# Loading the first adaLN weights ahead of the tokens, and another order of block 1's branches

## The chip, the cores and the metric

The kernel runs on one core of a Trainium2 chip. A core has TensorE (PE in the profile, with its weight loads as PEld), VectorE (DVE), ScalarE (ACT), GpSimd (POOL) and SyncE (SP, which here only issues DMAs). The metric is the device time of one execution in microseconds (us). Three runs of the kernel before took 3515.60, 3515.91 and 3515.91 us; the median is 3515.91.

## The reference

Three blocks follow each other on 512 tokens of width 1024, all in float32.

```
def reference(x, c, ctx, c_ctx, ...):
    x = first_block(x, c, ctx, c_ctx, ...)
    x = second_block(x, ...)
    return third_block(x, c_3, ...)

# first_block, one layer
sh1, sc1, g1, sh2, sc2, g2 = split(silu(c) @ w_ada + b_ada, 6)
p = modulate(rms_norm(x, norm1_g), sh1, sc1) @ w_in       # 10272 columns
q, k, v, a_dn, r, conv_in, sgu_in, gate_logit = split(p)
o = gla_bidir(q, k, v, gates(a_dn), s_f, s_b)             # 4 heads, chunks of 64, both directions
y_a = (rms(o) * gla_norm_g * silu(r)) @ w_o_gla           # attention branch
hc = depthwise_conv(c1 * sigmoid(c2))                     # 31 taps within rows of 64
y_b = silu(layer_norm(hc)) @ w_o_conv                     # convolution branch
y_c = (su * sp) @ w_o_sgu                                 # spatial gating branch
y = sigmoid(gate_0) * y_a + sigmoid(gate_1) * y_b + sigmoid(gate_2) * y_c
x = x + g1 * (y @ w_out)
x = x + g2 * swiglu(modulate(rms_norm(x), sh2, sc2))
```

The states `s_f` and `s_b` come from 256 context tokens with a modulation of their own. The second block has two layers, each a feed-forward, a mixer of two kinds of causal attention (8 heads with forget gates, 4 differential heads) and a feed-forward. The third block is one layer: a gated linear recurrence and block-sparse attention beside each other, one output projection.

## The kernel before

**Main products.** Activations lie as eight blocks of 128 features x 512 tokens. Each float32 factor is split into a rounded part `hi` and the rest `lo`, and a main product of a 128x128 weight tile is three matmuls: weight hi by activation hi, hi by lo, lo by hi (`mm3`; a triple below, 4408 in the kernel). The profile shows two of them with `whi` and one with `wlo`.

**Weights.** They stream in chunks of 128x1024 (512 KB, eight triples each) over SP's queue into three buffers `wraw`; ScalarE rounds a chunk to `whi`, and VectorE (in some stages POOL for every other chunk) subtracts to `wlo`. `w_start` issues the first loads, `w_ensure` the rounding, `w_finish` the subtraction and the next load; `wnext` calls the last two as triples go by.

**What sets the order.** Every engine executes its instructions in the order in which the program issues them. That order is made when the kernel is built, by a planner: a clock (`k.clk`) adds up planned times from small cost functions (`cost_pe`, `cost_act`, `cost_dve`, `cost_pool`). The side work (attention heads, the convolution, norms) is written as generators. After every triple `tick` lets each of them go on; `yield from k.sync()` holds one back until TensorE's planned time has passed the planned end of its last operation. So the planned costs decide behind which triple a dependent side matmul stands in TensorE's row. A matmul that stands too early makes TensorE wait, since the row is in order; one that stands late only delays what hangs on it. `k.filler` is a generator that is asked when little else is due: in block 1 `conv_work`, which issues 8 channel blocks of 31 steps each on VectorE (`calm` lets it go on while VectorE's planned time is less than 1.5 us ahead).

**Block 1.** First the modulation: `Ada1` computes shift and scale in four pairs of 256 columns. Pair 0 is done on TensorE (`rows`: 8 matmuls with a 2-column stationary side, a copy, 4 transposes), pairs 1 to 3 on VectorE for the tokens (`step`: eight multiply-adds of 128x512, then `sums`, four matmuls with a column of ones). `warm(k, n)` issues n matmuls that compute nothing. Six columns of units (the convolution's first inputs, `first_units`) run over all eight blocks `m` while pairs 1 to 3 come in; then the rest of the convolution's inputs, queries, values and keys. Behind the keys the attention's generators start (`ctx_state`, `gla_heads` with two heads at a time, `conv_norm` for the layer norm behind the convolution), and the main units follow a list:

```
ORDER_1 = (some("r", range(KT)) + some("g", range(6), 1) + some("g", range(6), 0) + between(1, 6) + some("a", [0])
           + between(0, 6) + some("v", range(2)) + some("s", range(KT)) + some("g", range(6), 2) + between(2, 6))
```

`r` are the eight units of the attention's output gate, `(g, m, b)` a gate unit of branch b (0 attention, 1 convolution, 2 spatial gating), `p` a product of branch b, which needs all eight blocks of its source, `a` is a marker after which the gating of the attention may be finished, `v` and `s` are the inputs of the spatial gating. `between(b, ahead)` alternates products with the gate units that are still missing. A unit is eight triples. The attention of a head (`gla_head`, `gla_dir`, `gla_gate`) is a chain over all engines: log-sigmoid on ScalarE, scans on VectorE, products with the decay on POOL, small matmuls on TensorE, and so on; `both` is a 128x4 product of chunk decays in it.

**Lines.** Nearly every instruction is recorded on the helper's line (L256 before, L260 in the changed kernel; DMAs L247 and L251), so rows are told apart by tiles: `wraw`, `whi`, `wlo` weights, `b` blocks in SBUF, `bk` PSUM banks, `pvt` a table of parameters (the convolution's taps among them), `cst` constants, `small` and `tinies` columns.

## Time and profile before

| | us |
|---|---|
| median of three runs | 3515.91 |
| the profiled execution | 3511.07 |
| its span in the trace | 3509.3 |
| TensorE busy | 3405.3 |
| VectorE busy | 1911.7 |
| ScalarE busy | 1351.7 |
| POOL busy | 720.5 |

The rows below come from the profiled execution. Busy time is the time in which an engine executes; "idle before" is its idle time just ahead of an instruction, put down to the engine whose semaphore came last. [...] Stages by time: 0 to 83 us the start with its modulation, to 271 us the convolution's inputs, queries, keys and values, to about 520 us the attention of block 1 (beside its main units), to 840 us the branch products, and block 1's feed-forward behind them; the mixers of block 2 at 1640 to 1900 us and 2660 to 2900 us; block 3's mixer at 3290 to 3480 us.

### The profile page before, as it was taken

What the parts mean: (1) busy time and instruction counts of PE and PEld (TensorE: products, weight loads), DVE (VectorE), ACT (ScalarE), POOL (GpSimd) and SP (SyncE); (2) the same over time, 40 slices, a digit from 0 to 9 for tenths busy, and PEclk for the clock granted to TensorE, in tenths of its full rate; (3) what the DMA queues carried; (4) which work ended last, traced back from release to release, by engine and by line L of the source; (5) the groups of instructions that cost most, each with busy time, mean ns of one, the idle gap of its engine ahead of it and who ended that gap; (6) DMA issues with size and microseconds to landing.
All of it is one profiled execution on the core that took longest, in us unless ns stands there. A gap on an engine that the chain in (4) does not pass through costs nothing.

```text
span 3509.3 us, 39437 instructions
## 1 busy us (share of the span) xinstructions
PE 3405.3 (97%) x15210; PEld 2763.3 (79%) x15210; DVE 1911.7 (54%) x3010; ACT 1351.7 (39%) x2176; POOL 720.5 (21%) x564
## 2 busy tenths in 40 slices
PE   7998889999999999999999999999999999999999
PEld 5886678887888888887778888888887778888777
DVE  5899865655333365433686443344335774433566
ACT  3324462223322332324764222233227653232474
POOL 0004231222000101103452110011016331111362
PEclk9998999999999999999999999999999999999999
DMA  6211114543322244232122222322332123222221
GB/s 209 93 56 55 48 49 149 181 156 102 102 98 99 99 159 164 97 117 98 55 68 80 99 97 96 96 96 97 107 108 72 60 68 108 96 96 96 72 79 55
DMA packets 110189, 344.99 MB, mean 98 GB/s; under 512 B 13425, under 2 KB 13681, under 8 KB 110001
## 3 DMA queue, kind: packets, MB, share of 16 engines
q1 hardware_dynamic: 84960, 296.78, 25.2%
q10 hardware_dynamic: 23760, 41.50, 3.7%
q0 software_dynamic: 1280, 4.20, 0.4%
q8 instruction: 119, 1.95, 0.2%
q14 instruction: 70, 0.57, 0.1%
HBM read 336.13 MB, written 6.29 MB: 98 GB/s over the span
## 4 chain that ended last, share of the span: by engine, by line
PE 52%; DVE 4%; ACT 2%; POOL 1%; issue 1%; DVEq 0%; POOLq 0%; ACTq 0%
PE bk L256 52%; DVE b L256 3%; ACT b L256 1%; DVE tinies L256 1%; POOL b L256 1%; POOL wlo L256 0%; DVE wlo L256 0%; ACT whi L256 0%; ACT L251 0%; ACT bk L256 0%; ACT tinies L256 0%; DVE small L256 0%; DVEq L256 0%; POOLq L256 0%; ACTq L256 0%
## 5 line engine op out<-in xcount | busy, mean ns | idle before, releaser
L256 PE MATMUL bk<-b,whi 128*128 128x512 f32 (+1 forms) x8048 | 2514.7, 394 | 6.8 <-ACT whi L256 3.4
L256 PEld LDWEIGHTS bk<-b,whi 128*128 128x128 f32 x8048 | 1506.7, 190 | 323.3 <-issue 9.6
L256 PE MATMUL bk<-b,wlo 128*128 128x512 f32 (+1 forms) x4024 | 1575.4, 391 | 6.7 <-DVE wlo L256 5.9
L256 POOL TENSOR_TENSOR b<-b,b 128x512 f32<-128x512 f32 (+2 forms) x381 | 528.4, 1395 | 2391.1 <-DVE b L256 1189.4
L256 DVE TENSOR_TENSOR wlo<-wraw,whi 128x1024 fp32r<-128x1024 f32 x495 | 643.8, 1303 | 528.8 <-ACT whi L256 528.5
L256 PEld LDWEIGHTS bk<-b,wlo 128*128 128x128 f32 x4024 | 762.2, 189 | 170.1 <-DVE wlo L256 8.8
L256 ACT CAST whi<-wraw 128x1024 fp32r<-128x1024 f32 x542 | 568.0, 1049 | 739.8 <-PE bk L256 442.8
L256 ACT CAST b<-b 128x512 fp32r<-128x512 f32 (+3 forms) x286 | 176.0, 618 | 523.9 <-POOL b L256 369.9
L256 DVE TENSOR_TENSOR b<-bk,b 128x512 f32<-128x512 f32 (+6 forms) x324 | 208.1, 659 | 253.7 <-PE bk L256 212.9
L256 DVE TENSOR_TENSOR b<-b,b 128x512 fp32r<-128x512 f32 (+3 forms) x250 | 184.7, 745 | 251.0 <-ACT b L256 248.9
L256 PE MATMUL bk<-b,b 128*128 128x128 f32 (+9 forms) x1056 | 250.4, 354 | 33.2 <-POOL b L256 20.4
L256 ACT ACTIVATE b<-b 128x512 f32<-128x512 f32 (+1 forms) x259 | 153.4, 608 | 308.7 <-DVE b L256 273.1
L256 PEld LDWEIGHTS bk<-b,b 128*128 128x128 f32 (+3 forms) x1056 | 174.1, 193 | 109.9 <-issue 36.0
L256 PE MATMUL bk<-whi,b 128*128 128x512 f32 x768 | 248.4, 397 | 4.0 <-ACT b L256 2.2
L256 DVE SCALAR_TENSOR_TENSOR b<-b,pvt,b 128x392 f32<-128x392 f32 (+7 forms) x296 | 229.0, 778 | 33.3 <-ACT b L256 26.4
L256 PEld LDWEIGHTS bk<-whi,b 128*128 128x128 f32 x768 | 145.6, 190 | 36.6 <-DVE b L256 3.0
L256 DVE SCALAR_TENSOR_TENSOR b<-b,small,b 128x512 f32<-128x512 f32 (+1 forms) x178 | 148.0, 833 | 20.8 <-ACT b L256 15.5
L256 POOL TENSOR_TENSOR wlo<-wraw,whi 128x1024 fp32r<-128x1024 f32 x47 | 116.0, 2467 | 202.3 <-ACT whi L256 175.7
L256 PE MATMUL bk<-wlo,b 128*128 128x512 f32 x384 | 150.8, 393 | 0.0
L256 PE MATMUL bk<-cst,b 128*128 128x128 f32 (+1 forms) x776 | 111.5, 271 | 36.3 <-DVE b L256 25.3
L256 PEld LDWEIGHTS bk<-cst,b 128*128 128x128 f32 x776 | 98.9, 168 | 60.4 <-DVE b L256 31.8
L256 ACT ACTIVATE b<-bk 128x512 f32<-128x512 f32 (+2 forms) x170 | 97.2, 572 | 111.6 <-PE bk L256 109.9
(93 smaller groups left out, 1233.9 us busy)
## 6 DMA issues: line engine op xcount, KB each, us to landing
wraw<-in_wst SPq DMA_DIRECT2D x542, 512.0 KB, 3.3
b<-in_ada1r ACTq DMA_DIRECT2D x64, 256.0 KB, 4.4
b<-in_ada ACTq DMA_DIRECT2D x48, 256.0 KB, 4.1
b<-in_ada SPq DMA_DIRECT2D x32, 256.0 KB, 5.5
xpark<-b ACTq DMA_DIRECT2D x16, 256.0 KB, 2.0
b<-xpark POOLq DMA_DIRECT2D x16, 256.0 KB, 5.2
b<-in_x SPq DMA_DIRECT2D x8, 256.0 KB, 5.2
b<-in_x ACTq DMA_DIRECT2D x8, 256.0 KB, 4.5
```

The costliest lines, as they stand in the source:

```text
L256: return f(*a, **kw)
```

## The change

The diff in full:

```diff
--- before.py
+++ after.py
@@ -225,13 +225,17 @@
     n = width(out)
     if op == "reciprocal":
         return 0.07 + 6.4e-3 * n
+    if op == "tensor_tensor_scan":
+        return 0.03 + 2.2e-3 * n
+    if op == "scalar_tensor_tensor" and n > 300 and len(tuple(out.shape)) == 3:
+        return 0.2 + 1.1e-3 * n
     if op in ("tensor_scalar", "memset"):
         return max(0.2, 0.1 + 0.7e-3 * n)
     return max(0.2, 0.08 + 1.05e-3 * n)
 
 
 def cost_pool(op, out, a, kw):
-    return 0.06 + (1.0e-3 if op == "memset" else 2.3e-3) * width(out)
+    return 0.06 + 1.0e-3 * width(out) if op == "memset" else max(0.5, 0.1 + 2.7e-3 * width(out))
 
 
 class Engine:
@@ -1876,8 +1880,8 @@
     return o
 
 
-ORDER_1 = (some("r", range(KT)) + some("g", range(6), 1) + some("g", range(6), 0) + between(1, 6) + some("a", [0])
-           + between(0, 6) + some("v", range(2)) + some("s", range(KT)) + some("g", range(6), 2) + between(2, 6))
+ORDER_1 = (some("r", range(KT)) + some("g", range(KT), 0) + some("g", range(KT), 1) + some("a", [0]) + between(0, KT)
+           + between(1, KT) + some("v", range(2)) + some("s", range(KT)) + some("g", range(6), 2) + between(2, 6))
 
 
 def plan1():
@@ -1980,9 +1984,15 @@
     def rows(self, q):
 
         k, nc = self.k, self.k.nc
-        b, row = k.bank(), k.blk()
+        b = k.bank()
         for t in range(KT):
             nc.tensor.matmul(b[0:2], lhsT=self.sc[:, t, :], rhs=self.ws[q][t].f, start=t == 0, stop=t == KT - 1)
+        k.free(self.ws.pop(q))
+        return b
+
+    def turn(self, q, b):
+        k, nc = self.k, self.k.nc
+        row = k.blk()
         nc.scalar.copy(row.f[0:2], b[0:2])
         k.unbank(b)
         b = k.bank()
@@ -1991,7 +2001,7 @@
         for c in range(2):
             self.finish(q, c, b[:, c:8:2])
         k.unbank(b)
-        k.free(row, self.ws.pop(q))
+        k.free(row)
 
     def step(self, q, c, t, acc):
         ve, w, s = self.k.nc.vector, self.ws[q][t].f, self.sc[:, t, c:c + 1]
@@ -2138,7 +2148,7 @@
                          start=True, stop=True)
     pairs = lambda ap: ap.rearrange("p (b c t) -> p b c t", c=2, t=64)
     chunk = dec.rearrange("p (b c) -> p b c", c=2)
-    nc.gpsimd.tensor_mul(both, chunk[:, :, 0], chunk[:, :, 1])
+    nc.vector.tensor_mul(both, chunk[:, :, 0], chunk[:, :, 1])
     f, l = pairs(kd.f)[:, :, s], pairs(qe.f)[:, :, 1 - s]
     nc.gpsimd.tensor_mul(f, f, chunk[:, :, 1 - s:2 - s].to_broadcast([P, 4, 64]))
     nc.gpsimd.tensor_mul(l, l, chunk[:, :, s:s + 1].to_broadcast([P, 4, 64]))
@@ -2431,18 +2441,23 @@
     w = "w_in"
     st = dict(q={}, k={}, v={}, r={}, o={}, ck={}, cv={}, s0=[k.blk() for _ in range(4)], cdone=0, hdone=0,
               conv={}, hc={}, yb={}, z={}, sv={})
+    ada = Ada1(k)
+    ada.load(0)
     for m in range(KT):
         x.append(k.blk())
         nc.sync.dma_start(x[m].f, k.a["x"][:, m, :])
-    ada = Ada1(k)
-    ada.load(0)
+    k.w_start(1)
+    ada.load(1)
     k.w_start()
-    ada.load(1)
-    warm(k, 7)
+    row = ada.rows(0)
+    warm(k, 3)
     k.clk.t = k.clk.c["dve"] = k.clk.c["act"] = 6.0
     acc = sumsq(k, [x[m].f for m in range(KT)], S, nc.vector)
     lt, ly = rms_cols(k, acc.f, S, EPS1)
-    ada.rows(0)
+    ada.turn(0, row)
+    k.w_ensure(0)
+    k.w_finish(0)
+    warm(k, 3)
     bcb = bc_rows(k, ly)
     hx = []
 
@@ -2456,8 +2471,6 @@
         k.free(x[m])
 
     prepare(0)
-    k.w_ensure(1)
-    k.w_finish(1)
     prepare(1)
     ada.load(2)
     cols = k.bank()
@@ -2474,7 +2487,7 @@
             summed = k.clk.t
         for n, c0 in enumerate(first_units()):
             k.main_mm3(fb[n], k.wnext(w, 0, m, c0), (hx[m][0].r, hx[m][1].r), m == 0, m == KT - 1)
-            if m % 2 == 1 and n == 1 and q < 4:
+            if m % 2 == 1 and n == 3 and q < 4:
                 k.clk.t = summed
                 ada.sums(cols[:, 4 * q:4 * q + 4], gacc)
                 ada.finish(q, 0, cols[:, 4 * q:4 * q + 4])
```

In words. (1) The planned costs of a scan, of a wide fused operation over three dimensions (the convolution's steps) and of every POOL operation change, and with them the places of side work in all three blocks. (2) In block 1 all 16 gate units of the attention and the convolution branch stand behind `r`, and the products of the attention branch come ahead of the convolution branch's. (3) The loads of ada pair 0 are issued ahead of the tokens, one weight chunk ahead of pair 1 and the other two behind it; the rows of pair 0 are the first work of TensorE; there are 3 + 3 warming matmuls instead of 7; the second weight chunk is finished later and the column sums of pairs 1 to 3 stand behind two more triples. (4) `both` moves from POOL to VectorE, 8 instructions.

The next two pieces are VectorE's row in the start of block 1: token blocks (`b_5` and `b_6` before, `b_13` and `b_14` after) times the broadcast norm in a bank, subtractions for their lo parts, weight halves (`wlo`), and the steps of ada pair 1 (into `b_51`, `b_52`). Before:

```order
L256 TENSOR_TENSOR b_5_95<-b_5_95,bk_70 128x512
L256 TENSOR_TENSOR b_40_222<-b_5_95,b_39_221 128x512
L256 TENSOR_TENSOR wlo_86<-wraw_80,whi_83 128x1024
L256 TENSOR_TENSOR wlo_87<-wraw_81,whi_84 128x1024
L256 TENSOR_TENSOR b_6_97<-b_6_97,bk_70 128x512
L256 TENSOR_TENSOR b_42_234<-b_6_97,b_41_233 128x512
L256 TENSOR_SCALAR b_51_254<-b_21_134,small 128x512
L256 SCALAR_TENSOR_TENSOR b_51_254<-b_22_135,small,b_51_254 128x512
```

After, from the second token block on; the half `wlo_86` and the second warming's memset stand ahead of this:

```order
L260 TENSOR_TENSOR b_14_117<-b_14_117,bk_71 128x512
L260 TENSOR_TENSOR b_43_232<-b_14_117,b_42_231 128x512
L260 TENSOR_SCALAR b_52_252<-b_21_132,small 128x512
L260 SCALAR_TENSOR_TENSOR b_52_252<-b_22_133,small,b_52_252 128x512
L260 SCALAR_TENSOR_TENSOR b_52_252<-b_23_134,small,b_52_252 128x512
L260 SCALAR_TENSOR_TENSOR b_52_252<-b_24_135,small,b_52_252 128x512
L260 SCALAR_TENSOR_TENSOR b_52_252<-b_25_136,small,b_52_252 128x512
L260 SCALAR_TENSOR_TENSOR b_52_252<-b_26_137,small,b_52_252 128x512
L260 SCALAR_TENSOR_TENSOR b_52_252<-b_27_138,small,b_52_252 128x512
L260 SCALAR_TENSOR_TENSOR b_52_252<-b_28_139,small,b_52_252 128x512
L260 TENSOR_TENSOR wlo_87<-wraw_81,whi_84 128x1024
L260 TENSOR_TENSOR wlo_88<-wraw_82,whi_85 128x1024
```

The half `wlo_87` of the second weight chunk stood ahead of the steps and stands behind the eighth of them.

The next two are TensorE's row during block 1's attention, where the sum over all convolution outputs (`cst` by the block with the accumulated sum, four matmuls of one column) stands. Before (this is behind triple 426, counted from the first):

```order
L256 MATMUL bk_73<-b_197_2574,b_183_2327 128x256
L256 MATMUL bk_69<-b_117_1365,b_185_2329 128x256
L256 MATMUL bk_67<-b_198_2577,b_187_2376 128x256
L256 MATMUL bk_72<-b_118_1366,b_189_2378 128x256
L256 MATMUL bk_71<-cst,b_111_1107 128x1 x4
L256 MATMUL bk_68<-b_64_317,whi_85 128x512
L256 MATMUL bk_68<-b_65_318,whi_85 128x512
L256 MATMUL bk_68<-b_64_317,wlo_88 128x512
```

After (behind triple 499):

```order
L260 MATMUL bk_71<-b_242_3066,b_217_2803 128x256
L260 MATMUL bk_73<-b_128_1623,b_219_2805 128x256
L260 MATMUL bk_66<-b_243_3069,b_224_2849 128x256
L260 MATMUL bk_72<-b_127_1622,b_226_2851 128x256
L260 MATMUL bk_67<-b_65_325,whi_85 128x512
L260 MATMUL bk_67<-b_66_326,whi_85 128x512
L260 MATMUL bk_67<-b_65_325,wlo_88 128x512
L260 MATMUL bk_68<-cst,b_112_1143 128x1 x4
L260 MATMUL bk_67<-b_67_331,whi_85 128x512
```

The side matmuls of attention heads (`b` by `b`) stand ahead of the sum in both; the sum stands 73 triples further on in the row.

The last two are the end of the attention in block 3, TensorE's row from its last attention matmuls (into `bk_73` before, `bk_70` after) to the next triples. Before:

```order
L256 MATMUL bk_73<-b_1808_22540,b_1634_21061 128x256
L256 MATMUL bk_73<-b_1809_22541,b_1634_21061 128x256
L256 MATMUL bk_73<-b_1808_22540,b_1632_21055 128x256
L256 MATMUL bk_73<-b_1809_22541,b_1632_21055 128x256
L256 MATMUL bk_68<-b_1779_22279,whi_83 128x512
L256 MATMUL bk_68<-b_1780_22280,whi_83 128x512
L256 MATMUL bk_68<-b_1779_22279,wlo_86 128x512
L256 MATMUL bk_70<-b_1760_22176,whi_84 128x512
L256 MATMUL bk_70<-b_1761_22177,whi_84 128x512
L256 MATMUL bk_70<-b_1760_22176,wlo_87 128x512
```

After:

```order
L260 MATMUL bk_71<-b_1807_22578,whi_85 128x512
L260 MATMUL bk_71<-b_1808_22579,whi_85 128x512
L260 MATMUL bk_71<-b_1807_22578,wlo_88 128x512
L260 MATMUL bk_70<-b_1811_22600,b_1635_21065 128x256
L260 MATMUL bk_70<-b_1812_22601,b_1635_21065 128x256
L260 MATMUL bk_70<-b_1811_22600,b_1633_21059 128x256
L260 MATMUL bk_70<-b_1812_22601,b_1633_21059 128x256
L260 MATMUL bk_73<-b_1813_22631,whi_85 128x512
```

Behind the last attention matmul 33 triples are left before and 20 after, to the end of the program.

## Rows read from the trace of the kernel before

**Rows 1.** page, busy time by engine: share, instructions

```profile
PE 3405.3 (97%) x15210; PEld 2763.3 (79%) x15210; DVE 1911.7 (54%) x3010; ACT 1351.7 (39%) x2176; POOL 720.5 (21%) x564
```

**Rows 2.** windows: length, busy us and instructions by engine, granted clock, DMA

```profile
83.20:271.20 188.00, 187.01 (x895) 156.87 (x894) 168.39 (x261) 50.81 (x75) 0.00 (x0) 1.00 0.24 78
271.20:400.00 128.80, 102.16 (x438) 79.46 (x438) 124.94 (x148) 56.42 (x119) 63.35 (x53) 0.87 0.14 47
400.00:519.50 119.50, 106.18 (x520) 87.91 (x519) 85.10 (x152) 78.96 (x147) 31.60 (x32) 0.93 0.15 49
...
1640.00:1900.00 260.00, 251.22 (x1103) 189.06 (x1103) 187.73 (x459) 166.67 (x365) 127.18 (x100) 0.96 0.19 64
...
2660.00:2900.00 240.00, 232.28 (x1027) 174.40 (x1026) 177.62 (x442) 157.35 (x355) 117.57 (x96) 0.96 0.19 64
...
3290.00:3480.00 190.00, 183.91 (x836) 143.83 (x835) 127.60 (x254) 128.28 (x230) 87.70 (x68) 0.98 0.21 69
```

**Rows 3.** waits of TensorE, 271.2 to 519.5 us: total, times, longest

```profile
PE bk L256 <- POOL b L256: 19.3, 10, 3.3
PE bk L256 <- DVE b L256: 16.9, 4, 7.9
```

**Rows 4.** groups of VectorE, 160 to 480 us: count, busy us, mean ns, idle

```profile
L256 DVE SCALAR_TENSOR_TENSOR b<-b,pvt,b 128x480 f32<-128x480 f32 (+14 forms) x222 | 168.0, 757 | 6.5
L256 DVE TENSOR_TENSOR wlo<-wraw,whi 128x1024 fp32r<-128x1024 f32 x33 | 43.4, 1314 | 2.0 <-ACT whi L256 2.0
L256 DVE TENSOR_TENSOR b<-b,b 128x512 f32<-128x512 f32 (+3 forms) x31 | 26.1, 857 | 3.4 <-ACT b L256 2.9
L256 DVE TENSOR_TENSOR_SCAN b<-cst,b 128x256 f32<-128x256 f32 (+1 forms) x16 | 20.4, 1282 | 1.3 <-POOL b L256 1.3
```

**Rows 5.** groups of TensorE, 271.2 to 519.5 us, matmuls with lo weights

```profile
L256 PE MATMUL bk<-b,wlo 128*128 128x512 f32 (+1 forms) x176 | 72.4, 412 | 0.6 <-DVE wlo L256 0.6
```

**Rows 6.** timeline of TensorE: start, length, idle before and releaser

```profile
422.54 0.39 PE L256 MATMUL bk<-b,wlo 128*128 128x512 f32 x1
...
423.89 0.39 PE L256 MATMUL bk<-b,wlo 128*128 128x512 f32 x1
...
454.57 1.87 PE L256 MATMUL bk<-cst,b 128*128 128x1 f32 x8 [7.92 <-DVE b L256]
```

**Rows 7.** POOL's groups by form, 160 to 480 us and 1900 to 2640 us

```profile
L256 POOL TENSOR_TENSOR b<-b,b 128x512 f32<-128x512 f32 x32 | 49.7, 1577 | 61.9 <-ACT b L256 46.0 <-DVE b L256 15.9
...
L256 POOL TENSOR_TENSOR b<-b,b 128x512 f32<-128x512 f32 x58 | 74.8, 1290 | 645.3 <-DVE b L256 399.9 <-ACT b L256 245.4
```

**Rows 8.** timeline of the start, all engines

```profile
6.39 4.17 SPq L247 DMA_DIRECT2D b<-in_ada  x8
...
6.61 4.26 ACT L256 ACTIVATE b<-b 128x512 f32<-128x512 f32 x8
...
7.40 8.56 PE L256 MATMUL bk<-b 128*128 128x512 f32 x14 [7.40 <-DVE b L256]
...
16.67 7.03 PE L256 MATMUL bk<-b,small 128*2 128x512 f32 x16
...
29.24 2.36 DVE L256 TENSOR_TENSOR wlo<-wraw,whi 128x1024 fp32r<-128x1024 f32 x2 [0.24 <-ACT whi L256]
...
29.26 1.22 PE L256 MATMUL bk<-b,whi 128*128 128x512 f32 x2 [3.41 <-ACT whi L256]
...
40.59 1.87 PE L256 MATMUL bk<-cst,b 128*128 128x1 f32 x8 [3.84 <-DVE b L256]
```

**Rows 9.** waits of TensorE, 3290 to 3480 us

```profile
PE bk L256 <- POOL b L256: 4.9, 1, 4.9
```

**Rows 10.** groups by form, 3290 to 3480 us, all engines

```profile
L256 POOL TENSOR_TENSOR b<-b,b 64x512 fp32r<-64x512 f32 x16 | 22.5, 1409 | 1.1
...
L256 DVE TENSOR_TENSOR b<-bk,b 64x512 f32<-64x512 f32 x7 | 4.8, 685 | 0.9 <-ACT b L256 0.7
...
L256 ACT COPY b<-bk 64x512 f32<-64x512 f32 x7 | 4.1, 582 | 4.1 <-PE bk L256 3.9
```

## The prediction

> **What bounds the kernel now.** I read the page first: TensorE is busy in 97% of the span [rows 1]. So only two things can be won: time in which TensorE waits, and time in which it runs at the lower of its two clocks. The windows say where that is [rows 2]. From 83.2 to 271.2 us TensorE is busy for 187.01 of 188 us at granted clock 1.00. In the next two windows, which are the attention of block 1, it is busy for 102.16 of 128.80 us and 106.18 of 119.50 us, at 0.87 and 0.93. These 248.3 us lose 39.9 us to idling. [...] At full clock without waits TensorE's work there would fill 208.3 - 25 = 183 us (up to 65 us lost). What it waits for there is POOL, 19.3 us, and DVE, 16.9 us [rows 3]. DVE is at its limit in the first of the two windows (124.94 of 128.80 us) and POOL is half full. The list of DVE's groups says with what: 222 steps of the depthwise convolution at 757 ns are 168 us, weight halves 43.4 us [rows 4]. So the stretch is bound by VectorE, because the convolution must be finished there: the matmul that sums its result stands early. The three attention stages of the later blocks lose less: 8.8, 7.7 and 6.1 us idle at clocks 0.96 to 0.98 [rows 2].
>
> **Block 1: other units during attention.** The window holds 176 triples (the row of lo weights counts one per triple) [rows 5], and at full clock one takes 0.68 us (two last matmuls of triples start at 422.54 and, two triples on, at 423.89 us) [rows 6]. In the order of before the sum over the convolution stands behind triple 426, that is 90 triples into the attention, and the first product (of the convolution branch) at triple 496. After the change the sum stands behind triple 499, and the first product (now of the attention branch) at triple 528; triples counted from the first main product. All products of a branch need all eight blocks of its source. So what has to be done by VectorE before TensorE may go on is spread over 192 triples (336 to 528) rather than 90, and the wait for the convolution's sum should go.
>
> What does VectorE do in those 192 triples? I counted the instructions between the two weight halves in the order of after and multiplied by the durations of before: 131 convolution steps x 757 ns = 99.2 us; 25 weight halves x 1314 = 32.9 us; 20 products of 512 at 857 = 17.1 us; 16 scans x 1282 = 20.5 us [rows 4]; the other 90 or so, small ones, about 42 us by their shapes, an estimate. Sum 212 us. TensorE's own work there is 183 + 16 x 0.68 = 194 us. So VectorE stays the limit, but by 18 us, not by 60. At the 97% at which the trace shows it at most (124.94 of 128.80) that takes 219 us. The convolution starts the stretch with 22 steps less behind it (101 instead of 123), so VectorE was less loaded before and may enter up to two weight chunks ahead; I take 5 us of these 11. That gives 214 us. Before, the same 192 triples took 248.3 + 16 x 0.68 = 259 us. **Gain: 45 us**, of which I count 44, since the sum over the convolution's squares comes later too.
>
> Its bounds: if TensorE's 194 us plus 10 us of short waits decide, 55 us are won. If POOL's chain (19.3 us of waits [rows 3]) isn't loosened by more triples between, 45 - 20 = 25.
>
> Heads 2 and 3 now run beside convolution steps. In the trace POOL's 512-wide products take 1577 ns in the stretch in which VectorE is full and 1290 ns in a stretch without convolution [rows 7]. Some 16 such products stand in heads 2 and 3: 16 x 0.29 = 4.6 us on POOL, which lies beside main products. I cost it at nothing; uncovered it is 5 us. [...]
>
> The eight tiny products that move from POOL (with `both`) to VectorE relieve POOL's chain by less than 1 us per head and add the same order to VectorE; counted in the 42 us above.
>
> **The start.** The first ada pair goes ahead of the tokens on SP's queue. Its eight loads take 4.17 us to issue, so the last token block lands 4 to 5 us later and the squares end at about 16 us instead of 10.87 [rows 8]. TensorE does the rows of pair 0 (7.03 us) meanwhile rather than after 14 halves of warming (8.56 us) [rows 8], of which 6 are left ahead of the sums. From 17 us: the sums, the inverse root and finishing the rows, 4 us together, as before; a weight half 1.2 and a memset 0.5 that the second warming waits for; that warming 6/14 x 8.56 = 3.7; broadcast, multiplication and scaling 2.7, as before. That makes the first main product start at 29.1 us instead of 29.26. The weight half of the second chunk, which stood ahead of the ada steps, now stands behind the eight of them (before, both halves start at 29.24 us [rows 8], ahead of the steps); TensorE needs it at triple 8. The steps start earlier by its 1.2 us and by the first half's 1.2 us, and the column sum, which came at 40.59 [rows 8], comes two main products later. From there VectorE paces the remaining pairs as before. Net 0, between -2 and +2 us.
>
> **Blocks 2 and 3: the planner's costs.** Higher planned costs for POOL, scans and the wide fused operations make the planner put dependent side matmuls later in TensorE's row. This takes a wait away where the real time was longer than the planned one. There is little to take: POOL's one wait in block 3 is 4.9 us [rows 9], and the two layers of block 2 idle for 16.5 us for all reasons; I put the upper gain at 10 us. What it costs is that the attention's side work ends nearer to the end of its cover. In block 3 the last attention matmul has 20 triples behind it instead of 33, and these 20 include the ones that need its result. That chain behind it is a copy of 0.58 us, an addition of 0.69 us, a POOL product of 1.41 us [rows 10], a cast and a subtraction of about 0.6 and 0.7 us: 4 us, with the clock's fall 5. The two layers of block 2 end their attention 4 and 6 triples later, with the same kind of chain: 3 us each. And in layer 2, 67 side matmuls now stand in one cluster between two triples where 21 stood; I put 1 us on it. **Sum +12 us.** The bounds: -10, and +40 where the chains of all three stages stand open at half clock and the waits of before remain (their whole loss today is 22.6 us idle and, by the clock of the windows, up to 24 us [rows 2]).
>
> **The sum.** -44 + 0 + 12 = -32 us against the profiled execution's 3511.07 us: 3479. That execution lies 4.8 us below the median of 3515.91; so 3484 on the median's footing. I take 3482.
>
> **The rivals.**
> A. The later blocks lose nothing or gain: the side matmuls that were moved had slack anyway. For it: TensorE idles only 3% to 4% there. Against it: the cover behind block 3's attention shrinks from 33 to 20 triples. Then 3516 - 45 = 3471, or 3461 with all POOL waits gone. I put 3468.
> B. Attention in block 1 stays bound more tightly than VectorE's sum says, by POOL's chains or by waits of VectorE for ACT in order: gain 25, and +12 later: 3503. For it: POOL waits are the larger part today. Against it: they were counted while VectorE, which feeds POOL, was late.
> C. Slower: VectorE works in order, and the change puts some 39 more convolution steps between the operations of heads 2 and 3: 39 x 0.757 = 30 us. If the last heads' outputs, ready at about 522 us before, come that much later, the first attention product, which needs all eight of them, holds TensorE until 552 us instead of passing at 485 us; before, TensorE was at this triple at 530. That is +22, and +12 from the later blocks makes 3550. It decides from outputs later than 518 us on. Against it: the heads start at the same triple, and the stretch ahead of them is shorter by the waits that go.
> D. The change doesn't move the end: what block 1 gives, the later blocks and the hole at 840 us take. 3513.
>
> **How the numbers follow.** What a measurement of this kernel can tell from no change is 0.2%, 7 us. Forecast 0.44, A 0.22, B 0.23, C 0.06, D 0.05. Forecast and A are faster by more than that, and of B all but 0.02: faster 0.87; D and the rest of B are 0.07 the same; C is 0.06 slower. The range leaves out C, D and the end of A in which every gain comes together (55 won and 10 more): 3456 to 3507.
>
> **What would show it.** In the window of heads 0 to 3 the idle of TensorE must fall from 39.9 us to under 15 and the clock rise to 0.97 or more, with VectorE at about 95% over it; the wait of 7.92 us before the convolution's sum [rows 6] must be gone, and the first product of the attention branch start at 480 to 492 us. If it starts later than 505, B holds; later than 530, C. At the start the first main product stands within 2 us of 29.26. In block 3 the 4.9 us behind POOL stays or shrinks, and a new wait of 3 to 6 us on the last attention blocks appears ahead of the last 20 triples; if none appears there and the windows of block 2 idle as before, A holds. Wrong altogether would be a new long wait in block 2's clusters, of more than 10 us in one place.

## The result, and the profile after

The changed kernel takes 3492.94 us (median of four runs, 3489.29 to 3493.59) against 3515.88 us: a ratio of 0.9933, with an interval of 0.9916 to 0.995. It is faster by 23 us, more than the 7 us that can be told from no change. Forecast were 3482 us and a range of 3456 to 3507: the direction and the range hold, and the gain is two thirds of the 34 us forecast. The profiled execution took 3493.36 us with a span of 3491.6 us, against 3509.3 us.

To see where the time went I counted triples: each has one matmul with lo weights, 4408 in every trace, so the start of the n-th of them is a common ruler. The table gives the difference in its start, changed kernel minus before, in us.

| triple | where | before starts at | difference |
|---|---|---|---|
| 0 | first main product | 30.52 | +3.5 |
| 8 | first with the second weight chunk | 43.32 | +0.1 |
| 100 | all ada pairs done | 121.53 | +6.7 |
| 336 | the attention of block 1 begins | 271.86 | +5.5 |
| 480 | inside it | 489.64 | -48.4 |
| 528 | first product in the changed order | 532.04 | -22.3 |
| 560 | products under way | 553.80 | -18.9 |
| 1024 | block 1's feed-forward | 902.72 | -22.2 |
| 2300 | behind layer 1's mixer | 1891.24 | -24.8 |
| 3650 | behind layer 2's mixer | 2919.59 | -20.5 |
| 4407 | last | 3505.12 | -17.7 |

So the start loses 6.7 us, the attention of block 1 gives 24.4 us (336 to 560), the rest of block 1 another 3 us, and blocks 2 and 3 take 4.5 us back. The lateness of the first product is made up by triple 8; the 6.6 us that stay are lost between triples 8 and 100. These are the windows of that stretch, first before, then in the changed kernel (columns as in the next table of windows):

```profile
43.32:121.53 78.21, 72.46 (x318) 59.43 (x316) 56.46 (x86) 29.11 (x39) 0.00 (x0) 0.94 0.38 124
```

```profile
43.47:128.28 84.81, 78.26 (x325) 63.01 (x325) 58.36 (x89) 28.25 (x38) 0.00 (x0) 0.88 0.39 131
```

TensorE idles 6.6 us instead of 5.8; the other 5.8 us are busy time, some 5 us of it by the granted clock, 0.88 instead of 0.94 (an estimate from these two rows: 0.12 x 84.81 us less 0.06 x 78.21 us). The granted clock stands in the profile as a share of full speed. Of 6980 windows of 0.5 us in the kernel before, 6676 read 1.00 and 264 read 0.50; a value between is a mean over a window in which it changes. These are the windows of the changed kernel for the convolution's inputs, the two halves of block 1's attention and the three later mixers (the last three set 20 us earlier than those of before, as the stages are). The columns are as in [rows 2]: length, busy us of TensorE, its weight loads, VectorE, ScalarE and POOL with instructions, the granted clock, DMA share and GB/s.

```profile
83.20:271.20 188.00, 188.00 (x890) 157.70 (x890) 159.16 (x246) 54.94 (x80) 0.00 (x0) 1.00 0.25 84
271.20:400.00 128.80, 116.46 (x543) 93.84 (x542) 119.98 (x152) 62.95 (x129) 58.58 (x49) 0.95 0.17 56
400.00:519.50 119.50, 107.49 (x533) 87.70 (x531) 99.11 (x167) 68.55 (x131) 33.98 (x27) 0.97 0.18 60
1620.00:1880.00 260.00, 249.56 (x1116) 189.21 (x1115) 187.00 (x461) 164.80 (x364) 124.44 (x100) 0.98 0.20 67
2640.00:2880.00 240.00, 228.42 (x1010) 171.03 (x1008) 178.10 (x438) 153.88 (x350) 114.71 (x93) 0.96 0.19 62
3270.00:3460.00 190.00, 186.24 (x847) 146.07 (x846) 133.21 (x253) 123.47 (x224) 86.21 (x67) 0.99 0.20 68
```

In the attention's 248.3 us TensorE idles 24.3 us where it idled 39.9 [rows 2], the clock is 0.95 and 0.97 instead of 0.87 and 0.93, and VectorE is busy for 93% and 83%. The reader is to see that VectorE isn't full in the second half: something else holds TensorE there. Its waits in the same 248.3 us, which answer to [rows 3] (total, times, longest):

```profile
PE bk L260 <- POOL b L260: 9.8, 7, 3.4
PE bk L260 <- ACT b L260: 7.8, 2, 7.4
PE bk L260 <- DVE tinies L260: 3.6, 2, 3.4
PE bk L260 <- DVE wlo L260: 2.0, 1, 2.0
PE bk L260 <- DVE b L260: 1.0, 2, 0.9
```

The waits for POOL halved, those for blocks of VectorE all but went, and a wait of 7.4 us for ScalarE is new. In TensorE's timeline that wait stands before a group of 24 side matmuls, and the column sum that waited 7.92 us [rows 6] waits 0.85 us:

```profile
458.80 6.63 PE L260 MATMUL bk<-b,b 128*128 128x256 f32 x24 [7.42 <-ACT b L260]
...
512.34 1.05 PE L260 MATMUL bk<-cst,b 128*128 128x1 f32 x8 [0.85 <-DVE b L260]
```

That column sum is not the one over the convolution's outputs. It is the second of the layer norm behind the convolution (`conv_norm`), over the squares of the centred outputs, and stands behind triple 459 before and behind 531 after. The sum over the outputs, behind triple 426 before and 499 after, waits in neither kernel; the last convolution step ends at 406.0 and at 475.9 us. First before, then after:

```profile
408.04 0.95 PE L256 MATMUL bk<-cst,b 128*128 128x1 f32 x8
```

```profile
476.96 0.95 PE L260 MATMUL bk<-cst,b 128*128 128x1 f32 x8
```

In the start, TensorE's timeline answers to [rows 8]: the rows of pair 0, the first warming, the second one, the broadcast, the first main matmul, the first one with the second chunk's lo half, and the column sums.

```profile
5.92 8.52 PE L260 MATMUL bk<-b,small 128*2 128x512 f32 x16 [5.92 <-ACT small L260]
14.37 2.84 PE L260 MATMUL bk<-b 128*128 128x512 f32 x6
...
23.61 5.49 PE L260 MATMUL bk<-b 128*128 128x512 f32 x6 [4.32 <-DVE b L260]
28.89 1.32 PE L260 MATMUL bk<-cst,tinies 128*128 128x128 f32 x8
31.83 0.49 PE L260 MATMUL bk<-b,whi 128*128 128x512 f32 x1 [1.62 <-ACT b L260]
...
43.47 0.79 PE L260 MATMUL bk<-b,wlo 128*128 128x512 f32 x1 [2.76 <-DVE wlo L260]
...
45.34 0.84 PE L260 MATMUL bk<-cst,b 128*128 128x1 f32 x4
```

The second warming takes 5.3 us (23.61 to 28.89) for three matmuls of two passes each; the same six passes took 2.84 us in the first warming. It stands behind 4.32 us of idling, and its window shows a granted clock of 0.50; its passes start 0.85 to 1.01 us apart, those of the first warming 0.43 to 0.53 us.

```profile
24.00:29.00 5.00, 5.00 (x7) 1.90 (x7) 0.00 (x0) 0.00 (x0) 0.00 (x0) 0.50 0.98 324
```

### The profile page after: what moved, and what is told of

Its sections match the earlier page's. It is cut to its first block, busy times and chain, and to the rows that moved or that the text cites. A ratio compares the mean times of both kernels' runs of the same rounds, so it can differ in the third digit from the quotient of the medians.

```text
span 3491.6 us, 39420 instructions
## 1 busy us (share of the span) xinstructions
PE 3397.1 (97%) x15208; PEld 2756.7 (79%) x15208; DVE 1919.8 (55%) x3018; ACT 1350.2 (39%) x2178; POOL 717.3 (21%) x556
## 4 chain that ended last, share of the span: by engine, by line
PE 55%; DVE 3%; issue 1%; ACT 1%; POOL 1%; POOLq 0%; DVEq 0%; ACTq 0%
PE bk L260 55%; DVE b L260 2%; DVE tinies L260 1%; ACT b L260 1%; DVE wlo L260 0%; POOL b L260 0%; POOL wlo L260 0%; ACT whi L260 0%; POOLq L2834 0%; ACT bk L260 0%; ACT tinies L260 0%; DVE small L260 0%; DVEq L260 0%; POOLq L260 0%; ACT L255 0%
## 5 line engine op out<-in xcount | busy, mean ns | idle before, releaser
L260 PE MATMUL bk<-b,b 128*128 128x256 f32 (+8 forms) x1056 | 248.7, 354 | 17.3 <-ACT b L260 7.8
L260 DVE SCALAR_TENSOR_TENSOR b<-b,pvt,b 128x392 f32<-128x392 f32 (+7 forms) x296 | 237.1, 805 | 33.0 <-ACT b L260 26.4
L260 PE MATMUL bk<-whi,b 128*128 128x512 f32 x768 | 248.3, 398 | 2.6 <-ACT b L260 2.2
```

Source lines behind the costliest of these rows:

```text
L260: return f(*a, **kw)
```

## The experiments

"At triple n" is the start of that triple's lo matmul minus its start in the profiled execution of the kernel before.

**The list of units alone.** Edit, on the kernel before:

```diff
-ORDER_1 = (some("r", range(KT)) + some("g", range(6), 1) + some("g", range(6), 0) + between(1, 6) + some("a", [0])
+ORDER_1 = (some("r", range(KT)) + some("g", range(KT), 0) + some("g", range(KT), 1) + some("a", [0]) + between(0, KT)
...
```

> The kernel before with the new list of block 1's units alone (planned costs, start and the tiny product as before). Theory 'order': the gain of block 1's attention (25 us from triple 336 to 560) comes from the units that now lie over the attention, so this kernel takes about 3493 us, and its first products of block 1 begin some 25 us earlier than before. Rival 'costs': the gain comes from side matmuls being placed later by the planned costs; then this kernel takes 3508 to 3516 us.

Measured: 3520.38 us against 3519.03 us, ratio 1.0005 (0.9991 to 1.002). Nothing is gained: the difference is -1.7 us at triples 336 to 440 and -0.2 us at 528. Theory 'order' falls. The waits are those of before, and the sum over the convolution's squares waits as long:

```profile
PE bk L256 <- POOL b L256: 19.4, 11, 4.2
PE bk L256 <- DVE b L256: 18.6, 5, 8.4
```

```profile
452.83 1.86 PE L256 MATMUL bk<-cst,b 128*128 128x1 f32 x8 [8.40 <-DVE b L256]
```

The side matmuls stand behind the same triples as before, whatever units these triples belong to; the first product was never what TensorE waited for. The two sums stand behind triples 426 and 459 as before, so it is not the list that moves them.

**The planned costs alone.** Edit, on the kernel before (the move of `both` to VectorE goes with them):

```diff
+    if op == "tensor_tensor_scan":
+        return 0.03 + 2.2e-3 * n
+    if op == "scalar_tensor_tensor" and n > 300 and len(tuple(out.shape)) == 3:
+        return 0.2 + 1.1e-3 * n
...
-    return 0.06 + (1.0e-3 if op == "memset" else 2.3e-3) * width(out)
+    return 0.06 + 1.0e-3 * width(out) if op == "memset" else max(0.5, 0.1 + 2.7e-3 * width(out))
...
-    nc.gpsimd.tensor_mul(both, chunk[:, :, 0], chunk[:, :, 1])
+    nc.vector.tensor_mul(both, chunk[:, :, 0], chunk[:, :, 1])
```

> The kernel before with the new planned costs (scans, wide fused operations, POOL) and the tiny product on VectorE; list of units and start as before. Theory 'order': block 1's attention gains less than 8 us, blocks 2 and 3 lose 4 us as in the changed kernel: 3512 to 3520 us. Rival 'costs': 20 us gained in block 1's attention, 3497 to 3502 us.

Measured: 3521.70 us, ratio 1.0016 (1.0003 to 1.0028). The rival falls too, but the triples show something that neither theory had: from triple 336 to 480 this kernel wins 53.9 us, exactly as the changed kernel does, and at triple 496 it is 3.3 us behind. Triple 496 is the first product of the old list. What the costs moved out of the way piles up in front of it. The stretch of those 16 triples, 432.9 to 509.9 us, as a window, and TensorE's waits in it:

```profile
432.90:509.90 77.00, 44.95 (x214) 35.73 (x213) 65.09 (x120) 35.37 (x76) 19.07 (x16) 0.80 0.08 26
```

```profile
PE bk L260 <- ACT b L260: 16.9, 3, 7.4
PE bk L260 <- DVE b L260: 9.0, 6, 3.6
PE bk L260 <- DVE tinies L260: 4.5, 1, 4.5
```

TensorE works 45 of 77 us there, at a mean clock of 0.80, on side work that has no triples left to lie beside. So the gain needs both: the costs take TensorE's waits away by putting side matmuls later, and the list gives 32 more triples (528 instead of 496) and another branch first, so that later is still early enough. Which of these two things in the list matters was not tested apart.

**Both, with the old start.** Edit: the two diffs above together on the kernel before; loads, warming and the places of the second weight chunk and of the column sums stay.

> The changed kernel with the start as before (loads, warming, second weight chunk, place of the column sums). Theory: the start costs the 6.75 us by which the changed kernel is late at triple 100, nothing later gives them back: 3486 us. Rival: the lateness is taken up again by slack in block 1's attention, since the side work there is late for other reasons: 3491 to 3493 us.

Measured: 3489.49 us, ratio 0.9926 (0.9902 to 0.9951). At triple 100 -1.9 us, at 336 -3.1, at 560 -27.5, at 1024 -30.5, at the end -19.7. The attention gives the same 24.4 us as in the changed kernel, and the start's lead stays up to triple 1024: nothing takes it up. Over the whole program it is 3.5 us against the changed kernel, from two sets of runs; that alone would not tell 7 us from 0.

**The start alone.** Edit: the parts of the change in `Ada1` and `block1`, on the kernel before:

```diff
+    ada.load(0)
     for m in range(KT):
...
-    warm(k, 7)
+    row = ada.rows(0)
+    warm(k, 3)
...
+    k.w_ensure(0)
+    k.w_finish(0)
+    warm(k, 3)
     bcb = bc_rows(k, ly)
...
```

> The kernel before with the new start alone. Theory: 6 to 7 us slower than before, 3522 us; at triple 100 late by 6.75 us as in the changed kernel. Rival: part of the lateness comes from the planned costs in the start; then triple 100 is late by less than 4 us and the time is under 3520.

Measured: 3517.20 us, ratio 1.0008 (0.9992 to 1.0023). At triple 100 it stands at 124.07 us; the kernels with the old start, on the same chip, at 119.66 to 119.97. So the start costs 4.2 us here, between the two expectations, and the total can't tell it.

**Costs in block 1 alone.** Edit, on the kernel with the old start (POOL's cost reads the same flag):

```diff
-    if op == "tensor_tensor_scan":
+    if NEW[0] and op == "tensor_tensor_scan":
...
+        NEW[0] = True
         block1(k, x, n12)
+        NEW[0] = False
```

> The changed kernel with the start as before, and with the new planned costs in block 1 alone: blocks 2 and 3 are ordered as in the kernel before, block 1 as without the new start. Theory: the new costs cost 4 to 10 us in blocks 2 and 3, so this takes 3480 to 3485 us and is the fastest so far; from triple 1024 to the end it takes as long as the kernel before. Rival: the blocks' times differ from execution to execution by as much for one and the same order (the clock falls at other places), so it takes 3487 to 3492 us, as without the new start alone.

Measured: 3482.31 us (3479.96 to 3484.05), ratio 0.9911 (0.9894 to 0.9927). From triple 1024 to the end it takes 1.3 us less than before; with the new costs in blocks 2 and 3 the same stretch took 4.5 us (changed kernel), 9.3 (costs alone) and 10.8 us (old start) more. The theory holds by its number. The rival isn't empty: the kernel with the list alone has exactly before's order in blocks 2 and 3 and took 7.9 us more there. Seven traces in all have before's order there: five others (this one, the start alone and the three of the last part below) lie between 1.3 us less and 1.9 us more than before, and the list alone stands apart; the three with the new costs lie 4.5 to 10.8 us above before. The medians, each against its own runs of before, give 4.0 us between the old start with costs everywhere and this kernel, and 4.7 us between the changed kernel and the same one with the costs in block 1 alone (the first of the last part). So the costs in blocks 2 and 3 stand beside some 4 to 10 us lost, with a scatter of the same size in single executions. From triple 1024 on TensorE idles 34.3 to 36.4 us with the new costs and 28.8 to 34.3 us with before's order, some 3 us more on the mean. The granted clock, 0.986 to 0.990 against 0.986 to 0.991 on the mean of the stretch, scatters with the same rows: a loss of more than these 3 us isn't shown to come from the costs.

**One kind of cost at a time.** Edits, on the kernel with the old start: the first and then the second of these taken back.

```diff
-    if op == "tensor_tensor_scan":
-        return 0.03 + 2.2e-3 * n
-    if op == "scalar_tensor_tensor" and n > 300 and len(tuple(out.shape)) == 3:
-        return 0.2 + 1.1e-3 * n
...
-    return 0.06 + 1.0e-3 * width(out) if op == "memset" else max(0.5, 0.1 + 2.7e-3 * width(out))
+    return 0.06 + (1.0e-3 if op == "memset" else 2.3e-3) * width(out)
```

> The changed kernel with the start as before and the old planned costs of VectorE: of the costs only POOL's is new. In block 1 its side matmuls stand 12 triples earlier on the mean than with both. Theory: the waits for VectorE (the convolution's sum at triple 426 to 440) come back, some 15 to 25 us are lost against the kernel with both costs: 3505 to 3515 us. Rival: POOL's cost is what frees TensorE: 3489 to 3495 us.

Measured: 3517.17 us, ratio 1.0004 (0.9995 to 1.0014); from 336 to 560 it gains 3.0 us. Since `both` is on VectorE here too, its move, with the list, isn't what frees TensorE.

> The changed kernel with the start as before and the old planned cost of POOL: of the costs only VectorE's are new. In block 1 its side matmuls stand 5 triples earlier on the mean than with both. Theory: the waits for POOL come back, 5 to 10 us lost against the kernel with both costs: 3495 to 3500 us. Rival: 3489 us, nothing lost.

Measured: 3508.45 us, ratio 0.9979 (0.9969 to 0.999); from 336 to 560 it gains 20.9 us of the 24.4, and blocks 2 and 3 take 23.1 us back. So it is VectorE's costs that free TensorE in block 1. In the later blocks neither cost alone is better than both: POOL's alone takes 9.2 us back, and this kernel's order there is another one, and the worst. That order computes a wrong output, for a reason that no run here shows, so its times stand for the order alone.

**A thin convolution.** Edit, on the kernel with the old start; the planned cost of these steps is kept at that of the full ones. TensorE's row in block 1 stays as it was; some places of blocks 2 and 3 move too, so only the stretch below is read.

```diff
-            d = dst[:, :, max(0, -s):64 - max(0, s)]
-            e, c = src[:, :, max(0, s):64 - max(0, -s)], ...
+            d = dst[:, 0:2, max(0, -s):64 - max(0, s)]
+            e, c = src[:, 0:2, max(0, s):64 - max(0, -s)], ...
```

> The changed kernel with the start as before and with convolution steps over 2 of the 8 rows of 64 tokens (three quarters of the convolution are left out); the planned costs are kept, so that the row of every engine in block 1 is the same. It tells apart what holds TensorE in the attention of block 1 from triple 336 to 528 (232 us, 23 us idle). Theory 'load': VectorE's load does, and its contention with POOL; with some 60 us less of convolution the stretch takes 200 to 208 us and TensorE idles for less than 8 us. Rival 'chains': the side work's own chains over ScalarE, VectorE and POOL are longer than the planner thinks; the stretch stays at 222 us or more, with waits of 15 us and more.

Measured: 3456.90 us, ratio 0.9835 (0.982 to 0.9849). The stretch from triple 336 to 528, first with the full convolution, then with the thin one:

```profile
268.76:501.04 232.28, 208.88 (x993) 169.14 (x992) 205.21 (x289) 124.08 (x249) 92.70 (x76) 0.96 0.16 53
```

```profile
270.66:482.44 211.78, 202.50 (x994) 166.05 (x994) 167.12 (x288) 123.82 (x250) 81.10 (x76) 0.98 0.17 58
```

It goes from 232.3 to 211.8 us, TensorE's idle from 23.4 to 9.3 us, the clock from 0.96 to 0.98. That is 20.5 us by VectorE's load, and most of the remaining idle is still the same two waits:

```profile
PE bk L263 <- ACT b L263: 5.1, 2, 4.5
PE bk L263 <- POOL b L263: 3.9, 3, 2.2
```

Neither range was met (200 to 208 us; 222 or more). 'Load' comes nearer, though VectorE was busy for only 88% of the stretch (205.2 of 232.3 us). That its load binds not as a sum, but by making each link of the heads' chains late, is argued from this and not shown. 'Chains' holds for the rest, 4.5 us of it the wait for ScalarE.

**The start, taken apart.** All three have block 1's costs and the new list; the first has the whole new start.

> The changed kernel with the new planned costs in block 1 alone, and with the whole new start. Theory: the new start costs 4 us or more at triple 100 (in the kernel with the start alone: 124.0 us, in those with the old start: 119.8 us); so triple 100 at 124 to 128 us, and 3486 us against the 3482 us of the same kernel with the old start. Rival: the start's loss belongs to single executions; triple 100 at 120 to 122 us.

Measured: 3489.05 us, ratio 0.9932 (0.9914 to 0.995). Triple 100 at 126.21 us, against 120.71 with the old start: 5.5 us lost.

```diff
-    warm(k, 3)
     bcb = bc_rows(k, ly)
```

> As the kernel with the whole new start and block 1's costs, but without the three warming matmuls behind the sums of squares (and without their memset). Theory 'warming': they run at half clock (5.49 us instead of 2.6) ahead of the broadcast that the first multiplication waits for; without them the first main product starts 4 to 5 us earlier, at 26 to 27 us, and triple 100 is 2 to 3 us earlier than with them. Rival 'cold': without them the first products run at half clock for as long, and triple 100 is where it was.

Measured: 3481.90 us (3473.29 to 3487.53), ratio 0.9905 (0.9883 to 0.9926). Triple 100 at 117.41 us: 8.8 us earlier than with the second warming, and 3.3 us earlier than with the old start. Theory 'warming' holds, with more than it expected: 5.8 us are there at the first triple, and another 2.7 us come between triples 8 and 100. The broadcast comes at 21.55 us and the first main matmul at 25.04:

```profile
21.55 1.86 PE L265 MATMUL bk<-cst,tinies 128*128 128x128 f32 x8 [2.10 <-DVE tinies L265]
25.04 0.79 PE L265 MATMUL bk<-b,whi 128*128 128x512 f32 x1 [1.62 <-ACT b L265]
...
36.67 0.50 PE L265 MATMUL bk<-b,wlo 128*128 128x512 f32 x1 [1.54 <-DVE wlo L265]
```

The products do begin at a granted clock of 0.50, as 'cold' has it, but they are products:

```profile
24.00:28.00 4.00, 2.19 (x4) 1.45 (x5) 1.42 (x3) 2.44 (x3) 0.00 (x0) 0.50 0.93 284
28.00:32.00 4.00, 4.00 (x11) 3.08 (x10) 3.01 (x5) 2.69 (x4) 0.00 (x0) 0.50 0.98 367
```

```diff
     prepare(0)
+    k.w_ensure(1)
+    k.w_finish(1)
     prepare(1)
...
-            if m % 2 == 1 and n == 3 and q < 4:
+            if m % 2 == 1 and n == 1 and q < 4:
```

> As without the second warming, and the second weight chunk finished ahead of the ada steps, the column sums behind two products instead of four, as before: of the new start the order of the loads is left, the rows of pair 0 first, and three warming matmuls. Theory: the weight half behind the steps cost 1.5 to 3 us (wait of 2.76 us at triple 8) and this takes them back: triple 100 at 119 to 121 us, no later than with the old start. Rival: VectorE paces the start in any order and triple 100 doesn't move against the kernel without the second warming.

Measured: 3481.58 us (3475.90 to 3487.07), ratio 0.9906 (0.9884 to 0.9928). Triple 100 at 118.66 us, 1.2 us later than without this edit. The rival holds: the weight half behind the steps costs nothing. All of the new start's loss is its second warming. What is left of the new start (the order of the loads, the rows of pair 0 first, three warming matmuls instead of seven) gains 1 to 3 us against the kernels with the old start, which reach triple 100 at 119.66 to 121.65 us; these three things were not tested apart.

The kernels with costs in block 1 alone, with the old start or with the new one without its second warming, are the fastest with the whole convolution: 3481.6 to 3482.3 us, against 3492.94 us of the changed kernel and 3515.9 us of before (each beside its own runs of before).

## Why the prediction was right and where it was wrong

The bound was read rightly: the time was in block 1's attention, and it came from there. How it would be won was not read rightly, and the range held in part by luck: block 1 gave 16 us less than forecast and the start cost some 7 us that were not forecast, while the later blocks took 7.5 us less, and the median moved 5 us more than the two profiled executions.

**Block 1, -44 us forecast, 24.4 us found (27.7 with the rest of the block).** The size: I let VectorE run at 97% over the 192 triples and so took 214 us; it took 232.4 us, with VectorE at 88%. Two durations were means over unlike stretches. I had 757 ns for a convolution step from 160 to 480 us [rows 4]; of one shape it takes 717 ns ahead of the attention (160 to 265 us) and 877 ns in it (300 to 480 us):

```profile
L260 DVE SCALAR_TENSOR_TENSOR b<-b,pvt,b 128x480 f32<-128x480 f32 x7 | 5.0, 717 | 0.2
```

```profile
L260 DVE SCALAR_TENSOR_TENSOR b<-b,pvt,b 128x480 f32<-128x480 f32 x7 | 6.1, 877 | 0.2
```

And POOL's products, which I had at 1577 ns, take 1670 ns:

```profile
L260 POOL TENSOR_TENSOR b<-b,b 128x512 f32<-128x512 f32 x32 | 52.7, 1670 | 51.7 <-ACT b L260 30.6 <-DVE b L260 21.2
```

I left that at no cost, and looked at POOL's side alone. But 877 ns is itself a mean of two kinds of steps. Of the 108 steps in the 192 triples, 60 overlap no operation of POOL and take 676 ns on the mean, 744 at most; 48 overlap one and take 1203 ns, up to 1806. Counted against the lone steps of the same shape, that is 24 us of VectorE's time, an estimate; the kernel before loses 16 us so between the same triples. In the kernel with the thin convolution one step shows it. Of its shape seven take 332 ns ahead of the attention; this one starts 0.04 us after a product of POOL has started, lasts 1377 ns and ends 0.13 us after the product:

```profile
L263 DVE SCALAR_TENSOR_TENSOR b<-b,pvt,b 128x110 f32<-128x110 f32 x7 | 2.3, 332 | 0.2
```

```profile
416.55 1.29 POOL L263 TENSOR_TENSOR b<-b,b 128x512 f32<-128x512 f32 x1 [2.69 <-ACT b L263]
```

```profile
416.59 1.38 DVE L263 SCALAR_TENSOR_TENSOR b<-b,pvt,b 128x110 f32<-128x110 f32 x1
```

VectorE's work as a sum was as forecast, by two errors that cancel: 108 steps of 910 ns on the mean are 98 us, where I had 131 of 757 ns, 99 us (and 205 us busy in all, against my 212). So a sum couldn't show the delay; the links of the heads' chains came late, TensorE idled 23 us, and the granted clock was 0.96 over the stretch; with the thin convolution it idled 9.3 us at 0.98. The prediction's 183 us of TensorE's work at full clock, which stand in its 194, take 25 us off the busy time, (1 - 0.87) x 128.8 + (1 - 0.93) x 119.5 us by [rows 2]: an estimate, and no run shows this term. What the runs showed in its place is 209.1 us of busy time at 0.96 from triple 336 to 528 in the changed kernel, and 202.5 us at 0.98 with the thin convolution. Whether the chains would be in time if no step were held beside POOL, no run tests. My bound from below, 25 us won if POOL's chain isn't loosened, is what came: rival B's attention.

The attribution: the prediction gave this gain to the list of units and priced the costs in blocks 2 and 3 alone. The list alone gave nothing and the costs alone nothing. I had read the place of the convolution's sum (triple 499 instead of 426) from the order of the whole change, which was right for the sum and could not tell which edit had moved it: the costs did. And I had put the wait of 7.92 us [rows 6] down to that sum. It stood at the sum over the squares, at 454.57 us, 48 us behind the last convolution step. So before, TensorE didn't wait at the sum over the outputs, and this wait belongs to the chain behind the convolution.

**The start, 0 forecast between -2 and +2, +6.7 found** (4.2 to 6.7 in three traces). The term that was mis-sized is the second warming: I took 6/14 of 8.56 us and counted 3.7 us. That was a mean over passes of two lengths: in the kernel before the first six start 0.85 to 1.01 us apart and the last eight 0.43 us. The same six passes took 2.84 us in the changed kernel's first warming. The second ran at a granted clock of 0.50 behind 4.32 us of idling, 5.3 us, and the broadcast stood behind it; it also began at 23.61 us, where my sum gives 22.7. So the first main product started at 31.83 us and not at 29.1. What I had put at nothing is the clock behind it: from triple 8 on I let the start run "as before", and there the changed kernel lost 6.6 us, some 5 of them, by the estimate above, by the granted clock of 0.88 instead of 0.94. Without the second warming the first main product starts at 25.04 us, and triples 8 to 100 take 2.7 us less. The weight half behind the ada steps, which I weighed too, costs nothing.

**Blocks 2 and 3, +12 us forecast, +4.5 found in the profiled execution, 9.3 and 10.8 in two other kernels with the same costs.** The sign agrees in all three; single executions of one order scatter by as much, so the size stays open. As forecast, the wait of 4.88 us behind POOL in block 3 is gone and a new one stands ahead of the last triples, 3.38 us, for ScalarE (the 1 us that I added there for the clock's fall is shown apart by no run; between 3465 and 3491 us the granted clock is 0.93); and in layer 2 TensorE waits up to 4.9 us at once for VectorE:

```profile
3471.80 0.50 PE L260 MATMUL bk<-b,whi 128*128 128x512 f32 x1 [3.38 <-ACT b L260]
```

```profile
PE bk L260 <- DVE b L260: 7.6, 4, 4.9
```

**The sum** was -32 and came out at -17.7 us between the two profiled executions and -23 between the medians; the profiled execution of before lay 4.8 us under its median. Of the marks I had set, the idle of under 15 us and the clock of 0.97 in the attention's window were missed (24.3 us; 0.95 and 0.97), and the first product of the attention branch came at 509 us, where I had put 480 to 492 and named 505 as the point from which B holds; the first main product lay 2.6 us behind that of before, where I had allowed 2. So the time lies between the forecast and B: B's attention, with later blocks that cost less. C did not come: no output of heads 2 and 3 made TensorE wait at the product. POOL's products take 29% more than the 1290 ns of [rows 7]; with the thin convolution they take 1510 ns. One step of 332 ns that met a product of 1290 ns lasted 1377 ns, where half speed would make it 664. The price is smaller on POOL's side (380 ns more for a product on the mean, some 12 us over 32 products, an estimate from the two means) than on VectorE's, 24 us by the estimate above, which I had only inside my mean of 757 ns.

## What to carry to other kernels

Where a planner's costs decide how late side work stands, and a list of units decides how much cover it has, an edit to one can be worth nothing without the other: read from a ruler of main products, in each trace, where the lead that one of them makes is given back. A refitted cost moves the other stages too: here the kernels that have it only in the stage whose waits it was fitted to were the fastest. Warming matmuls can cost more than they give: put ahead of a broadcast on the critical chain, behind 4.32 us of idling, three of them ran at a granted clock of 0.50 themselves and took 5.3 us, and without them triple 100 came 8.8 us earlier. And split a mean duration by what runs beside the operation before you multiply by it: steps alone and steps held beside another engine are two prices, 676 and 1203 ns here.

## What the runs showed of the hardware

One order of instructions takes times that differ by several us: the kernel with the list alone took 7.9 us more than before over blocks 2 and 3 with the same rows on TensorE, VectorE, ScalarE and POOL there, and 25 runs of the kernel before on one chip went from 3503.98 to 3524.96 us, where the first four lay within 0.3 us. An edit of 5 us is settled by the ruler inside one stage, not by the total.

VectorE's convolution steps took longer where POOL's operations overlapped them: 676 ns alone and 1203 ns beside an operation of POOL in the changed kernel, 331 and 879 ns with the thin convolution. So a step beside POOL took some 0.5 us more on the mean, and as much where it is half as long.
